# A hybrid decoder step on one core: two more buffers for the weight stream in the first two pieces of the input projection, and the next piece of the activations made ahead of the weight splits

## The chip, the cores and the metric

The kernel runs on one core of a Trainium2 chip. The metric is the device time of one execution in microseconds (us), as the median of several runs. In rows of the profile the engines are PE (TensorE, matrix products; PEld is its loading of weights), DVE (VectorE), ACT (ScalarE), POOL (GpSimd) and SP (SyncE, which here only issues DMAs). "SPq" and "POOLq" are the queues of DMAs that SP and POOL issue. "L675" is line 675 of the kernel before.

## The reference

One layer is computed for 264 tokens: a prompt of 256 and eight samples of one token each, D = 2048, all in float32. Cut to what matters here:

```python
mod = silu(c) @ w_ada + b_ada                     # (2048) @ (2048 x 12288)
sh1, sc1, gt1, sh2, sc2, gt2 = split(mod, 6)
h = rmsnorm(x, g_pre_mix) * (1 + sc1) + sh1
z = h @ w_in                                      # (264 x 2048) @ (2048 x 15376)
(z_uv, hq, hf, hi, ...) = split(z, ...)
...                                               # three mixers, gates, w_branch, w_out
x = x + gt1 * rmsnorm(out, g_post_mix)
h2 = rmsnorm(x, g_pre_mlp) * (1 + sc2) + sh2
y2 = square(relu(h2 @ w_mlp_up)) @ w_mlp_down
x = x + gt2 * rmsnorm(y2, g_post_mlp)
```

The point for this change is the order of the first lines: `h` needs `sh1` and `sc1`, two sixths of `mod`, and so 33.5 MB of `w_ada` before the first product with `w_in` is complete.

## The kernel before, in words

**Products in three passes.** A float32 product is made of three matmuls in a faster format. Each weight is split into a high part `whi` (ACT casts it, L631) and a low part `wlo` (DVE subtracts, L635). The activations are split in the same way into `hh` and `hl`. Lines L675, L676 and L677 then multiply `whi` by `hh`, `whi` by `hl` and `wlo` by `hh`.

**The stream.** All weights but `w_ada` come through one list of *granules* of 512 KB, loaded by DMAs that SP issues in the list's order (L616 for paired loads, L623 for single ones). A load waits until a buffer is free; the tag `raw` has four of them. `Stream.ahead`, called after each granule's matmuls, puts into the program the splits of the granule three places on (`SPLIT_AHEAD`) and the loads up to five places on (`LOAD_AHEAD`). A split can run when its load has landed and PE is through with the granule three places back. Two further buffers with the tag `araw` are used later, by paired loads and by `w_ada`.

**The first phase** makes 20 groups of 256 columns of `w_in`. As `h` isn't there at once, the 16 tiles of K are cut into five *pieces* of 2, 2, 4, 4 and 4 tiles (`CHUNKS`). Piece 0 runs over all 20 column groups with K tiles 0 and 1, piece 1 with tiles 2 and 3, and so on; the partial sums are added up in SBUF. A granule of pieces 0 and 1 is two K tiles by 512 columns, ten granules a piece, called g0 to g9 and g10 to g19 below; a granule of the later pieces is four K tiles by 256 columns, g20 and on. Each granule has two PSUM accumulators in pieces 0 and 1, and `evict` moves them to SBUF: in piece 0 ACT copies the first (L862) and DVE the second (L864), later DVE adds them (L110).

**Making the next piece.** While a piece runs, the class `First` prepares the activations of the next one as a generator (`paced`), resumed once after each granule by `next(nxt, None)` (L877). Its steps are: the `w_ada` matmuls in batches of four load units (L315, 1.9 us each), a copy of their sums to SBUF (`sums`, L319 on ACT), then `rows`: transposes on PE (L326), the sums to `mod` and `A1` on DVE (L110, L530), and at the next steps `modulate` for two K tiles at a time. `modulate` scales on ACT (L454, two instructions), computes the eight sample columns on POOL (L450, L451), casts the high part on ACT (L116) and subtracts for the low part on DVE (L113). The next piece's first matmul needs the cast.

**What sets the order.** In the first phase the order on all five queues is the order in which the program is written. After a granule's matmuls that is: its copies out, then the splits and the loads of `ahead`, then one step of the generator. `LOAD_AT` says at which granule each load unit of `w_ada` for the next piece is put into POOL's queue (256 KB per DMA for piece 1, 512 KB for the later ones, L502). POOL issues in order, so a load that stands behind L450 waits for it. A batch of `w_ada` matmuls is put in three granules (`ADA_LEAD`) after its last load unit was.

**The very first granule** has its own code: `modulate_first` computes the sample columns of the first two K tiles on POOL (L465 to L468), the rest on ACT (L471) and DVE (L472, L113), and `first_granule` (L689) uses them.

## Time and profile before

| what | us |
|---|---|
| median of 3 runs (1806.27 to 1812.08) | 1808.13 |
| the profiled execution's own time | 1805.63 |
| its span | 1803.9 |
| PE busy / DVE busy / ACT busy / POOL busy | 1775.1 / 1183.0 / 1001.4 / 138.7 |
| L675, L676 and L677 together | 3824.6 of overlapping matmuls |
| mean granted TensorE clock | 0.999 |

PE is busy for 98% of the span, and the chain of work that ended last is PE for 91% of it. So the kernel is bound by PE, and what can be won without taking work from PE is the sum of its gaps and the time in which its clock is lowered. The views to read are therefore the stages of the first phase in windows, and inside them the timeline of PE, with what ended each of its waits. DMA moved 442 MB at a mean of 245 GB/s over the span, but more than that in the first phase, where `w_ada` and `w_in` are fetched together.

### The profile page before, as it was taken

Reading aid. Unit: us, or ns where it says so; the run is one execution under the profiler, and the core shown is the slowest. Engines: PE = TensorE matmul, PEld = TensorE weight load, DVE = VectorE, ACT = ScalarE, POOL = GpSimd, SP = SyncE. Lnnn points to the kernel's source line nnn. Section 1 sums busy time; section 2 is a strip of 40 time slices with the busy share of each in tenths; the row PEclk is TensorE's granted clock in tenths of the full one; section 3 lists DMA queues with packets and bytes.
Section 4 is the critical chain, followed back from the end, with each engine's and each line's share of the span. In section 5 each row is a group of like instructions: output and inputs, shape, how many; then the busy total and the mean of one; then the engine's idle time right before and its main releaser. Section 6 shows DMA issues by size and latency. Waiting matters only on the chain.

```text
span 1803.9 us, 42121 instructions
## 1 busy us (share of the span) xinstructions
PE 1775.1 (98%) x16970; PEld 1687.9 (94%) x16970; DVE 1183.0 (66%) x2077; ACT 1001.4 (56%) x1824; POOL 138.7 (8%) x228
## 2 busy tenths in 40 slices
PE   7999999999999999999999999999999999999998
PEld 5889989999999989999999989999999999999997
DVE  5566667787687695566555667545666666666666
ACT  5344454677857765654444666555454545454554
POOL 4222000101101102110000010000000000000000
PEclk9999999999999999999999999999999999999999
DMA  9987587689689688887877946776666666666663
GB/s 339 387 338 282 197 291 253 208 293 304 211 281 302 218 276 303 306 311 257 289 262 253 327 140 203 240 248 221 192 196 198 196 193 197 196 193 196 199 191 116
DMA packets 330181, 442.05 MB, mean 245 GB/s; under 512 B 14947, under 2 KB 276945, under 8 KB 329985
## 3 DMA queue, kind: packets, MB, share of 16 engines
q1 hardware_dynamic: 311872, 380.52, 63.8%
q0 software_dynamic: 17184, 57.85, 9.4%
q8 instruction: 133, 2.18, 0.5%
q10 hardware_dynamic: 928, 0.99, 0.2%
q14 instruction: 64, 0.52, 0.1%
HBM read 427.60 MB, written 11.70 MB: 244 GB/s over the span
## 4 chain that ended last, share of the span: by engine, by line
PE 91%; DVE 1%; ACT 1%; issue 0%; DMA 0%; ACTq 0%; SPq 0%; DVEq 0%
PE mm L675 28%; PE mm L676 27%; PE mm L677 27%; PE ada L383 3%; PE ada L315 1%; PE sm L709 1%; PE sm L897 1%; PE sm L716 1%; DMA araw<-in_w_ada_dram 0%; DVE wlo L635 0%; PE sm L1622 0%; PE sm L1253 0%; DVE b L113 0%; DVE b L1602 0%; PE sm L1004 0%
## 5 line engine op out<-in xcount | busy, mean ns | idle before, releaser
L675 PE MATMUL mm<-b,whi 128*128 128x264 f32 x4600 | 1283.4, 279 | 4.8 <-ACT b L116 3.4
L677 PE MATMUL mm<-b,wlo 128*128 128x264 f32 x4600 | 1270.6, 276 | 1.1 <-DVE wlo L635 0.6
L676 PE MATMUL mm<-b,whi 128*128 128x264 f32 x4600 | 1270.6, 276 | 0.7 <-DVE b L113 0.7
L635 DVE TENSOR_TENSOR wlo<-raw,whi 128x512 fp32r<-128x512 f32 x1136 | 770.8, 689 | 463.4 <-ACT whi L631 460.2
L631 ACT CAST whi<-raw 128x512 fp32r<-128x512 f32 x1136 | 693.0, 617 | 672.4 <-DVE wlo L635 328.7
L675 PEld LDWEIGHTS mm<-b,whi 128*128 128x128 f32 x4600 | 870.1, 189 | 45.1 <-issue 23.3
L676 PEld LDWEIGHTS mm<-b,whi 128*128 128x128 f32 x4600 | 870.3, 189 | 1.4 <-DVE b L113 1.1
L677 PEld LDWEIGHTS mm<-b,wlo 128*128 128x128 f32 x4600 | 870.1, 189 | 1.5 <-DVE wlo L635 0.8
L110 DVE TENSOR_TENSOR b<-b,mm 128x528 f32<-128x528 f32 (+1 forms) x137 | 95.7, 699 | 74.6 <-PE mm L677 67.0
L1790 POOL TENSOR_TENSOR gs<-b,G 128x16 f32<-128x16 f32 x1 | 0.2, 223 | 714.1 <-DVE b L110 714.1
L502 POOL DMA_DIRECT2D b<-in_w_ada_dram x64 | 46.4, 727 | 39.2 <-PE ada L315 30.1
L383 PE MATMUL ada<-araw,cT 128*32 128x512 f32 x296 | 40.9, 601 | 0.8 <-DMA araw<-in_w_ada_dram 0.8
L1154 POOL DMA_DIRECT2D out_dram<-st x32 | 23.6, 737 | 223.7 <-DVE st L1153 223.7
L315 PE MATMUL ada<-b,cT 128*32 128x256 f32 (+1 forms) x640 | 34.5, 355 | 1.4 <-DMA b<-in_w_ada_dram 1.2
L1151 ACT ACTIVATE st<-st,fs 128x128 f32<-128x128 f32 (+1 forms) x96 | 35.1, 430 | 0.0
L1153 DVE SCALAR_TENSOR_TENSOR st<-vbc,b,st 128x128 f32<-128x128 f32 (+1 forms) x96 | 32.4, 390 | 3.7 <-DMA vbc<-vs_d 1.4
L107 DVE TENSOR_TENSOR b<-b,b 128x512 f32<-128x512 f32 (+1 forms) x47 | 33.8, 741 | 1.6 <-ACT b L1265 0.8
L315 PEld LDWEIGHTS ada<-b,cT 128*32 128x32 f32 x640 | 18.2, 114 | 12.6 <-DMA b<-in_w_ada_dram 4.1
L383 PE MATMUL ada<-b,cT 128*32 128x512 f32 x216 | 26.2, 593 | 0.0
L113 DVE TENSOR_TENSOR b<-gt,b 128x528 fp32r<-128x528 f32 x32 | 22.7, 708 | 3.2
L113 DVE TENSOR_TENSOR b<-b 128x1024 f32<-128x1024 f32 (+1 forms) x24 | 24.3, 1017 | 0.0
L1676 ACT ACTIVATE b<-vt 128x528 fp32r<-128x528 f32 x32 | 22.9, 714 | 1.0
(366 smaller groups left out, 902.7 us busy)
## 6 DMA issues: line engine op xcount, KB each, us to landing
raw<-in_w_in_dram SPq DMA_DIRECT2D x231, 512.0 KB, 5.1
raw<-in_w_mlp_up_dram SPq DMA_DIRECT2D x128, 512.0 KB, 3.7
raw<-in_w_mlp_down_dram SPq DMA_DIRECT2D x128, 512.0 KB, 3.5
araw<-in_w_ada_dram SPq DMA_DIRECT2D x74, 512.0 KB, 6.1
b<-in_w_ada_dram SPq DMA_DIRECT2D x54, 512.0 KB, 6.5
b<-in_w_ada_dram POOLq DMA_DIRECT2D x48, 512.0 KB, 10.5
raw<-in_w_branch_dram SPq DMA_DIRECT2D x48, 512.0 KB, 5.4
raw<-in_w_out_dram SPq DMA_DIRECT2D x32, 512.0 KB, 4.5
```

Source lines behind the costliest of these rows:

```text
L107: V.tensor_tensor(o, a, b, op=ALU.mult)
L110: V.tensor_tensor(o, a, b, op=ALU.add)
L113: V.tensor_tensor(o, a, b, op=ALU.subtract)
L315: T.matmul(acc[32 * j:32 * j + 32, 0:n], cT[:, k, :], w[:, n * j:n * j + n], start=k == 0, stop=k == KT - 1)
L383: T.matmul(self.acc[32 * j:32 * j + 32, :], cT[:, k, :], ws[j // 2][:, j % 2 * 512:j % 2 * 512 + 512], start=k == 0, stop=k == KT - 1)
L502: queue.dma_start(w[:, i], w1[k * P:(k + 1) * P, :, self.k0 * P:(self.k0 + self.n) * P])
L631: self.last = [S.copy(hi, raw).ins, None]
L635: self.last[1] = V.tensor_tensor(lo, raw, hi.bitcast(F32), op=ALU.subtract).ins
L675: T.matmul(o, a, xh(k + j), start=first and j == 0, stop=False)
L676: T.matmul(o, a, xl(k + j), start=False, stop=False)
L677: T.matmul(o, b, xh(k + j), start=False, stop=last and j == n - 1)
L1151: S.activation(st[:, i, :], st[:, i, :], AF.Copy, scale=fs[:, h0 + i, b:b + 1])
```

## The change

Four things are changed, all in the code of the first phase.

1. **Buffers.** In `Stream.load` every third granule of two K tiles (`n == 2 and i % 3 == 2`) takes a buffer of the tag `araw` in place of `raw`. With four `raw` and two `araw` that makes six. `Stream.ahead` loads seven granules ahead in place of five as long as the granule two further on is also one of two K tiles. Both conditions also hold for the eight granules of the first 512 columns of `w_mlp_up`.
2. **Order.** `granule` and `first_granule` take a function `between`, called ahead of `ahead()`. It advances the step and resumes the generator. So the generator's step now stands ahead of the splits and loads; the transposes of x (L282) stay behind them.
3. **Load table.** In `LOAD_AT`, the last three load units of piece 1 are put in one granule sooner. Those of piece 2 begin a granule later (7 in place of 6) and end a granule sooner (13 in place of 14). So the last batch of each piece, and with it `sums`, `rows` and `modulate`, comes a granule sooner.
4. **The first samples.** Two of the four small operations of `modulate_first` go from POOL to DVE.

```diff
 LOAD_AT = (
     (),
-    (0, 0, 1, 1, 2, 3, 4, 5),
-    (6, 6, 7, 8, 8, 9, 10, 10, 11, 11, 12, 12, 13, 13, 14, 14),
+    (0, 0, 1, 1, 2, 2, 3, 4),
+    (7, 7, 8, 8, 9, 9, 10, 10, 11, 11, 12, 12, 12, 13, 13, 13),
     tuple(range(16, 32)),
...
         hs, ls = (apart(b)[:, :, :, NP // 2:NT // 2] for b in (hi, lo))
-        Q.tensor_tensor(d, xs[:, 0:2, :], A[:, 0:2, 1:NC], op=ALU.mult)
-        Q.tensor_tensor(hs, by_two(d), by_two(B[:, 0:2, 1:NC]), op=ALU.add)
+        mul(d, xs[:, 0:2, :], A[:, 0:2, 1:NC])
+        add(hs, by_two(d), by_two(B[:, 0:2, 1:NC]))
         Q.tensor_tensor(d, d, B[:, 0:2, 1:NC], op=ALU.add)
...
-            t = rawp.tile([P, n, width], F32, tag="raw", name=nm("raw"))
+            if n == 2 and i % 3 == 2:
+                t = rawp.tile([P, n, width], F32, tag="araw", name=nm("araw"), bufs=ADA_RAW)
+            else:
+                t = rawp.tile([P, n, width], F32, tag="raw", name=nm("raw"))
...
-            for i in range(self.at + SPLIT_AHEAD + 1, min(self.at + LOAD_AHEAD + 1, end)):
+            last = self.at + LOAD_AHEAD
+            if self.items[min(last + 2, end - 1)][2] == 2:
+                last += 2
+            for i in range(self.at + SPLIT_AHEAD + 1, min(last + 1, end)):
                 if i not in self.raw:
                     self.load(i)
...
             if done:
                 done(acc0)
+        if between:
+            between()
         stream[0].ahead()
...
         for acc in accs:
             done(acc)
+        between()
         stream[0].ahead()
...
+            def between():
+
+                step[0] += 1
+                if not final:
+                    next(nxt, None)
+
             load_due()
             if ci or gi:
-                granule(win, 0, n, begin[gi * gn][0], gn * CW, accs, hH, hL, k0, True, True, evict)
+                granule(win, 0, n, begin[gi * gn][0], gn * CW, accs, hH, hL, k0, True, True, evict, between)
             else:
-                first_granule(accs, evict)
-            step[0] += 1
+                first_granule(accs, evict, between)
             if ci == 0 and 2 * gi + 8 < KT:
                 x_transposed(2 * gi + 8)
-            if not final:
-                next(nxt, None)
-            else:
+            if final:
```

**ACT at the end of piece 0.** Before, with `gt` the copy of the sums, `whi` the splits, `L862` the copies of g8 and g9 out of PSUM, and `L454`/`L116` the modulation for piece 1:

```order
L631 CAST whi_771<-raw_652 128x512
L319 COPY gt_809<-ada_580 128x128
L862 COPY b_177<-mm_811 128x528
L631 CAST whi_843<-raw_693 128x512
L631 CAST whi_847<-raw_693 128x512
L862 COPY b_179<-mm_857 128x528
L631 CAST whi_887<-raw_735 128x512
L631 CAST whi_891<-raw_735 128x512
L454 ACTIVATE b_271<-b_271,mod,A_169 128x256 x2
L116 CAST b_331<-b_271 128x528
```

And now (the line numbers are those of the changed kernel; L634 is L631, L871 is L862):

```order
L319 COPY gt_759<-ada_571 128x128
L634 CAST whi_761<-raw_481 128x512
L634 CAST whi_765<-raw_481 128x512
L871 COPY b_175<-mm_771 128x528
L634 CAST whi_807<-raw_531 128x512
L634 CAST whi_811<-raw_531 128x512
L871 COPY b_177<-mm_817 128x528
L454 ACTIVATE b_271<-b_271,mod,A_169 128x256 x2
L116 CAST b_331<-b_271 128x528
L634 CAST whi_855<-araw_612 128x512
L634 CAST whi_859<-araw_612 128x512
L871 COPY b_179<-mm_865 128x528
```

The modulation (L454, L116) stood behind the copy of g9 and two more splits; it now stands behind the copy of g8, ahead of the splits.

**POOL around the samples of piece 1.** The DMAs fetch `w_ada` for piece 2; L450 and L451 are the sample columns of the modulation. Before:

```order
L502 DMA b_813<-in_w_ada_dram 128x2x512
L502 DMA b_815<-in_w_ada_dram 128x2x512
L502 DMA b_859<-in_w_ada_dram 128x2x512
L450 TENSOR_TENSOR b_271<-xsn_132,A_169 128x2x8
L451 TENSOR_TENSOR b_271<-b_271,mod 128x2x8
L502 DMA b_905<-in_w_ada_dram 128x2x512
```

And now:

```order
L502 DMA b_819<-in_w_ada_dram 128x2x512
L502 DMA b_821<-in_w_ada_dram 128x2x512
L450 TENSOR_TENSOR b_271<-xsn_132,A_169 128x2x8
L451 TENSOR_TENSOR b_271<-b_271,mod 128x2x8
L502 DMA b_867<-in_w_ada_dram 128x2x512
L502 DMA b_869<-in_w_ada_dram 128x2x512
```

Of the sixteen loads of piece 2, six stood ahead of L450 (the first three aren't shown) and ten behind it; now four stand ahead (two aren't shown) and twelve behind.

**SP at the start of the stream.** Before, from the first granule on:

```order
L623 DMA raw_204<-in_w_in_dram 128x512 x2
L623 DMA raw_207<-in_w_in_dram 128x2x512
L623 DMA raw_209<-in_w_in_dram 128x2x512
L623 DMA raw_386<-in_w_in_dram 128x2x512
L623 DMA raw_388<-in_w_in_dram 128x2x512
L623 DMA raw_390<-in_w_in_dram 128x2x512
```

And now:

```order
L626 DMA raw_204<-in_w_in_dram 128x512 x2
L626 DMA raw_207<-in_w_in_dram 128x2x512
L626 DMA araw_209<-in_w_in_dram 128x2x512
L626 DMA raw_386<-in_w_in_dram 128x2x512
L626 DMA raw_388<-in_w_in_dram 128x2x512
L626 DMA araw_390<-in_w_in_dram 128x2x512
```

The order of the loads is the same, but the third and the sixth go to the two other buffers, so six loads can be out before the first buffer comes free, where it was four.

More of the change, by code (lines that the diff above doesn't have):

```diff
@@ L663, in hybrid_step_kernel, with granule @@
     stream = []
-    def granule(w, k0, n, c0, width, accs, xh, xl, k, first, last, done=None):
+    def granule(w, k0, n, c0, width, accs, xh, xl, k, first, last, done=None, between=None):
         item, parts = stream[0].next()
@@ L679, in granule, with first_granule @@
                 done(acc0)
+        if between:
+            between()
         stream[0].ahead()
-    def first_granule(accs, done):
+    def first_granule(accs, done, between):
         item, parts = stream[0].next()
```

## The prediction

> **What bounds the kernel now.** I read the page's busy times first, then the first phase in windows of 20 us, then PE's timeline in the windows that lose time, then the engines that PE waited for. The page says that PE is the bound, and so only its gaps and its clock can be won:
>
> ```profile
> PE 1775.1 (98%) x16970; PEld 1687.9 (94%) x16970; DVE 1183.0 (66%) x2077; ACT 1001.4 (56%) x1824; POOL 138.7 (8%) x228
> ```
>
> The windows (length, busy time of PE, PEld, DVE, ACT, POOL, then granted clock, DMA share, GB/s) show where they are:
>
> ```profile
> 20.00:40.00 20.00, 18.73 (x221) 16.45 (x225) 13.71 (x25) 11.68 (x22) 11.79 (x19) 1.00 0.97 357
> 40.00:60.00 20.00, 19.72 (x252) 19.00 (x241) 10.91 (x17) 9.60 (x19) 5.67 (x8) 1.00 1.04 404
> 60.00:80.00 20.00, 16.21 (x154) 13.71 (x153) 11.50 (x21) 7.01 (x13) 9.84 (x15) 0.91 0.97 362
> 80.00:100.00 20.00, 19.87 (x204) 17.57 (x203) 14.67 (x26) 8.22 (x15) 1.06 (x3) 1.00 0.79 301
> ```
>
> Two things stand in them. From 60 to 80 PE is idle for 3.8 us and its clock falls to 0.91; and up to 80 the DMA engines are full (share 0.97 and more), so whatever starts sooner takes bandwidth from something else. PE's timeline at the border of pieces 0 and 1 (start, duration, then in brackets the idle time before and who ended it):
>
> ```profile
> 58.77 0.28 PE L675 MATMUL mm<-b,whi 128*128 128x264 f32 x1
> ...
> 60.01 0.28 PE L677 MATMUL mm<-b,wlo 128*128 128x264 f32 x1
> 63.71 0.38 PE L675 MATMUL mm<-b,whi 128*128 128x264 f32 x1 [3.42 <-ACT b L116]
> 64.45 0.38 PE L676 MATMUL mm<-b,whi 128*128 128x264 f32 x1 [0.36 <-DVE b L113]
> ...
> 65.28 0.43 PE L677 MATMUL mm<-b,wlo 128*128 128x264 f32 x1
> ...
> 68.70 0.28 PE L677 MATMUL mm<-b,wlo 128*128 128x264 f32 x1
> ```
>
> The last matmul of g9 starts at 60.01, the last of g10 at 68.70. Matmuls at full clock follow each other every 0.113 us (58.77 to 60.01 are eleven steps), so the 24 of g10 should take 2.71; they took 8.69. The border costs 5.98 us: 3.42 and 0.36 of waiting, the rest from slow matmuls after it (0.43 against 0.28).
>
> [...]
>
> Why the cast L116 came so late is seen on ACT, DVE and POOL:
>
> ```profile
> 58.86 1.14 ACT L631 CAST whi<-raw 128x512 fp32r<-128x512 f32 x2 [1.79 <-DMA raw<-in_w_in_dram]
> 59.91 0.59 ACT L862 COPY b<-mm 128x528 f32<-128x528 f32 x1
> 60.77 1.14 ACT L631 CAST whi<-raw 128x512 fp32r<-128x512 f32 x2 [0.27 <-DMA raw<-in_w_in_dram]
> 61.82 1.09 ACT L454 ACTIVATE b<-b,mod,A 128x256 f32<-128x256 f32 x2
> 62.99 0.66 ACT L116 CAST b<-b 128x528 fp32r<-128x528 f32 x1
> 60.95 0.18 DVE L530 SCALAR_TENSOR_TENSOR A<-mod,vec 128x18 f32<-128x18 f32 x1
> 61.22 0.21 POOL L450 TENSOR_TENSOR b<-xsn,A 128x16 f32<-128x16 f32 x1 [13.31 <-DVE A L530]
> ```
>
> ACT first waits for two weight loads and splits them (58.86 to 61.9), then modulates. A1 (L530) is late for the same reason: it stands behind a DVE half of a split. So a wait for DMA is handed on, through two engines' queues, to PE.
>
> **The change part by part.** First the border. The two weight splits leave the path, and the chain starts a granule sooner. L326 and A1 come after g7, so A1 is ready about 4 us before PE is through with g9; ACT's L454 and L116 come behind g8's copy and take 1.09 + 0.66 = 1.75 us (from the rows above), and DVE's L113 follows. g8's first accumulator is full half a granule, 1.35 us, after g8 starts; with the copy (0.59) the cast is ready 3.7 us after that start, and PE wants it 5.4 after it (two granules). That leaves 1.7 us of cover: **gain 5.98 us**. The bounds are 5.98 (all) and 0 (the splits are still ahead of it in some way). What is queued behind: the split of g11 now waits for the modulation, 1.75 us; its granule is used two granules, 5.4 us, later, behind a batch of `w_ada`. And `sums` (L319) now holds ACT, ahead of a split, until the batch on PE is done; that split too is used three granules, over 8 us, later.
>
> The border of pieces 1 and 2 has a smaller copy of the same thing:
>
> ```profile
> 101.38 0.72 DVE L113 TENSOR_TENSOR b<-b,b 128x528 fp32r<-128x528 f32 x1 [0.38 <-ACT b L116]
> 102.86 0.35 PE L675 MATMUL mm<-b,whi 128*128 128x264 f32 x1 [0.73 <-DVE b L110]
> 105.25 0.38 PE L676 MATMUL mm<-b,whi 128*128 128x264 f32 x1 [0.36 <-DVE b L113]
> ```
>
> DVE waits with L113 for ACT's cast, the eviction L110 waits behind it, and PE for the eviction. Both pairs of tiles are now made a granule sooner: **gain 1.0** (0 to 1.09).
>
> The start: the first product waits for the samples from POOL and the scaled rows from ACT.
>
> ```profile
> 24.25 0.18 DVE L530 SCALAR_TENSOR_TENSOR A<-mod,vec 128x18 f32<-128x18 f32 x1
> 24.53 1.14 ACT L471 ACTIVATE b<-b,mod,A 128x256 fp32r<-128x256 f32 x2
> 24.59 0.21 POOL L465 TENSOR_TENSOR sqs<-xsn,A 128x16 f32<-128x16 f32 x1 [18.50 <-DVE A L530]
> 24.88 0.76 POOL L466 TENSOR_TENSOR b<-sqs,mod 128x16 fp32r<-128x16 f32 x1
> 25.69 0.49 PE L689 MATMUL mm<-b,whi 128*128 128x264 f32 x2 [0.40 <-ACT b L471]
> 24.87 0.68 DVE L635 TENSOR_TENSOR wlo<-raw,whi 128x512 fp32r<-128x512 f32 x1
> ```
>
> POOL ends at 25.64, ACT's first half at 25.1, so POOL was the later one, though the row names ACT. On DVE two operations of about 0.2 (as L530) end at 24.85, so PE can start at 25.1, 0.55 sooner. But DVE's own chain is pushed back by 0.4, and its `wlo` then ends at 25.95, where PE, four matmuls after its start, would want it at 25.55. **Gain 0.3** (-0.2 to 0.55).
>
> Now the costs: `w_ada` batches that PE reaches sooner than their loads land. The transposes, the batches on PE, and landing times (count, KB each, us from issue to landing; the first pair of rows is the DMAs issued at about 31.4 and 40.6, the eighth and the last of piece 1; then a weight load issued at 39.1; then loads of piece 2 issued at 62.0 and 71.4):
>
> ```profile
> 38.66 0.60 PE L282 MATMUL sm<-cst,b 128*128 128x128 f32 x4
> 39.19 1.96 PE L315 MATMUL ada<-b,cT 128*32 128x128 f32 x64
> 52.62 1.96 PE L315 MATMUL ada<-b,cT 128*32 128x128 f32 x64
> 91.29 1.93 PE L315 MATMUL ada<-b,cT 128*32 128x256 f32 x32
> ...
> 26.29 7.31 POOL L502 DMA_DIRECT2D b<-in_w_ada_dram  x10
> ```
>
> ```profile
> b<-in_w_ada_dram POOLq DMA_DIRECT2D x2, 256.0 KB, 8.8
> b<-in_w_ada_dram POOLq DMA_DIRECT2D x2, 256.0 KB, 8.0
> raw<-in_w_in_dram SPq DMA_DIRECT2D x1, 512.0 KB, 12.4
> b<-in_w_ada_dram POOLq DMA_DIRECT2D x1, 512.0 KB, 5.3
> b<-in_w_ada_dram POOLq DMA_DIRECT2D x2, 512.0 KB, 12.0
> ```
>
> Batch 1 of piece 1 needs its eighth DMA at three quarters of the 1.96 us, 40.65; it landed at 31.4 + 8.8 = 40.2, with 0.45 to spare. Now PE comes there 0.3 (start) and 0.53 (the transposes stand behind it) sooner, at 39.8. POOL starts its DMAs 0.9 sooner, as two operations (0.21 and 0.76) are gone. Against it stand two more weight loads of 0.52 MB in flight, 1.05 MB, at 404 GB/s (second window) up to 2.6 us. The wait is between 0 and 2.2. I take **0.5**: the window from 20 to 40 isn't full (357 against 404 GB/s, 0.9 MB), and that room nearly holds them.
>
> Batch 2 moves from 52.62 a granule sooner, to about 48.9 less what the start gained, and needs its last DMA at 50.4; it landed at 48.6. With the same shift it holds: 0 (0 to 0.8).
>
> Piece 2: of its loads twelve in place of ten stand behind L450, which moves from 61.2 to about 55. The first landed 5.3 after its issue, at 67.3; one of the last at 71.4 + 12.0 = 83.4. That is nine loads in 16.1 us, 293 GB/s. By that rate the twelve would land from 60.5 to 80.2; by what the window from 40 to 60 leaves `w_ada` (404 less four weight loads in 12.4 us, 169 GB/s: 235) until 85.1. PE reaches the last batch at 91.29 less 2.7 (a granule) less 6.3 (the shift), 82.3, and needs its last load at 83.7. The wait is 0 to 1.4; nearer the first, since the stream's six buffers are full by then and it only loads what is consumed: **0.5**.
>
> The MLP's eight granules are the last part. The two `araw` buffers are taken there by weights, and `w_ada` has to come after them:
>
> ```profile
> 959.41 0.34 SPq L346 DMA_DIRECT2D araw<-in_w_ada_dram  x1
> 1050.28 56.17 SPq L623 DMA_DIRECT2D raw<-in_w_mlp_up_dram  x14
> 1126.32 1.06 PE L383 MATMUL ada<-araw,cT 128*32 128x512 f32 x8
> ```
>
> This load was issued 167 us ahead of its use. It now comes behind about ten of these fourteen, at some 1095, 31 us ahead, and even 12.4 for landing leaves 19: 0. If that cover were gone, PE would wait there once.
>
> The sum: 5.98 + 1.0 + 0.3 - 0.5 - 0.5 = 6.3 us. The profiled execution took 1805.63 (its span 1803.9 and 1.7 around it), so it would take 1799.3. It is faster than every run shown; from the median, 1808.13, the same gain gives **1801.8**, 0.35% less. About 0.3%, 5.4 us, is what a measurement of this kernel tells from no change.
>
> **The rivals.** *The wait only moves.* The batches wait for their DMAs by the upper bounds, 2.2 + 0.8 + 1.4 = 4.4 in place of 1.0, and 2.9 are left: 1805.2. For it speaks the DMA share of 1.04, against it that from 80 to 100 the bus has room (share 0.79).
>
> *The stream takes the bus (slower).* Place: the last batch of piece 1, and then that of piece 2. With six weight loads in flight in place of four, 169 becomes up to 169 x 6/4 = 253, and 404 - 253 leaves 151 GB/s for `w_ada`. Eight DMAs of 0.262 MB took from 40.2 to 48.6, 250 GB/s; at 151 the second eight take 13.9, 5.5 later: 54.1 against 50.4, a wait of 3.7. Eleven loads of 0.524 MB behind the first, at 60.5 + 3.7, take 38.2 and end at 102, against 83.7 + 3.7: 15 more, with twice 1.8 of slow clock (0.09 of 20 us). The sum is 7.3 - 3.7 - 15 - 3.6, 15 slower: 1823. The point from which it decides is a share of `w_ada` of about 200 GB/s. Against it: the stream is held by its buffers, and once these are full it can't take more than PE consumes.
>
> [...]
>
> *The change doesn't do it.* ACT's splits of g9 and g10 still wait for DMA ahead of the modulation, and A1 is as late as before relative to PE. Then 0 to 1 is won: 1807.5. Against it: the six buffers put the loads two granules ahead.
>
> **How the numbers follow.** My forecast 0.60 (gain over 5.4); the wait only moves 0.18; the change doesn't do it 0.05; the stream takes the bus 0.17, of it 0.07 near equal turns with no difference and 0.10 slower. So faster 0.60, same 0.30, slower 0.10. The low end is all gains with no costs, 7.6, and 4 for the spread of the runs: 1796.5. The high end takes in the first and third rival and the mild form of the second: 1809.5.
>
> **What would show it.** Right: no wait on L116 at the border of pieces 0 and 1, g10 in 2.7 us, no slow clock after the start, no gap at the next border, the first L689 at about 25.1 to 25.4. Wrong: PE waiting at L315 for DMA `w_ada` for more than 2 us, or weight splits that wait longer for their loads than before.

## The result, and the profile after

| | before | after |
|---|---|---|
| median of 5 runs, us | 1808.13 | 1800.21 |
| lowest to highest, us | 1806.23 to 1812.08 | 1798.0 to 1801.41 |
| span of the profiled execution, us | 1803.9 | 1799.6 |
| the profiled execution's own time, us | 1805.63 | 1801.41 |

The changed kernel is faster: the ratio is 0.9959, with an interval of 0.9947 to 0.9971. The ratio is worth 7.4 us, between 5.2 and 9.6, and the two medians lie 7.9 apart. The prediction was 1801.8, in a range of 1796.5 to 1809.5.

Line numbers of the changed kernel are higher: L681, L682 and L683 are the L675, L676 and L677 of before; L634 and L638 are the splits L631 and L635; L871 and L873 the copies out of PSUM L862 and L864; L697 the first granule's L689. L110, L113, L116, L315, L450, L454 and L530 keep their numbers.

The first phase of the changed kernel, in the same windows of 20 us (length, busy time of PE, PEld, DVE, ACT, POOL, then granted clock, DMA share, GB/s):

```profile
20.00:40.00 20.00, 18.87 (x188) 16.62 (x187) 13.60 (x27) 12.71 (x25) 10.89 (x16) 1.00 1.05 400
60.00:80.00 20.00, 20.00 (x215) 17.26 (x217) 15.14 (x25) 8.29 (x15) 8.10 (x12) 1.00 1.02 391
```

From 60 to 80 PE was busy for 16.21 us at a clock of 0.91; it is busy for all 20.00 now, at 1.00. The first window moves 400 GB/s in place of 357, which is 0.86 MB more in 20 us.

The border of pieces 0 and 1, on PE (g9's last matmul, then the first and the last of g10, and the batch behind it) and on ACT, with A1 on DVE:

```profile
60.91 0.28 PE L683 MATMUL mm<-b,wlo 128*128 128x264 f32 x1
61.12 0.38 PE L681 MATMUL mm<-b,whi 128*128 128x264 f32 x1
...
63.81 0.28 PE L683 MATMUL mm<-b,wlo 128*128 128x264 f32 x1
64.01 0.64 PE L315 MATMUL ada<-b,cT 128*32 128x256 f32 x8
```

```profile
57.17 0.60 ACT L871 COPY b<-mm 128x528 f32<-128x528 f32 x1 [0.96 <-PE mm L683]
57.67 1.09 ACT L454 ACTIVATE b<-b,mod,A 128x256 f32<-128x256 f32 x2
58.85 0.68 ACT L116 CAST b<-b 128x528 fp32r<-128x528 f32 x1
56.55 0.18 DVE L530 SCALAR_TENSOR_TENSOR A<-mod,vec 128x18 f32<-128x18 f32 x1
```

g10 follows g9 without a wait: 2.90 us from g9's last matmul to g10's, in place of 8.69. The cast L116 is ready at 59.53, 1.6 us ahead of the matmul that wants it at 61.12. ACT now waits for PE ahead of its copy (0.96), and no longer for a load. Its longest waits from 27 to 65, the one before and then two after (line, who is waited for, us in total, times, longest):

```profile
ACT whi L631 <- DMA raw<-in_w_in_dram: 13.0, 8, 2.2
```

```profile
ACT b L871 <- PE mm L683: 8.4, 8, 3.3
ACT gt L319 <- PE ada L315: 2.7, 1, 2.7
```

Before, ACT waited for loads 8 times, 13.0 us in all; now only for PE.

What PE waits for from 26 to 110 in the changed kernel (line, who is waited for, us in total, times, longest):

```profile
PE mm L681 <- ACT b L871: 0.4, 1, 0.4
PE mm L681 <- DVE b L873: 0.3, 1, 0.3
PE mm L681 <- DVE b L110: 0.2, 1, 0.2
```

The first two stand at g1, ahead of its first and its second accumulator, right behind the start, and the second of them is new. No batch of `w_ada` waits for its loads.

**A measure that start and end do not blur.** The span fell by 4.3 us, and the median of the runs by 7.9. Two things lie between. A1 of the first piece, the end of all that happens before the first product, came at 25.38 in place of 24.25. And PE lost time in a place that the change doesn't touch: at 663.53 it waits for 2.01 us ahead of a matmul of L718, and the profile shows nothing that it waited for. Before, the same wait is 0.65. Over the thirteen profiles of this case the time from the fourth piece's first batch to the end of the span lies between 1693.6 and 1697.9 (1694.5 before, 1696.1 after, and the longest with the MLP's part undone), though nothing but that part acts there. So I compare kernels by a *stretch*: from A1 (the first L530) to the first `w_ada` batch of the fourth piece. All of the change but the MLP's loads acts inside it. Its end before (its start, 24.25, stands in the prediction), and then both ends after:

```profile
109.39 1.93 PE L315 MATMUL ada<-b,cT 128*32 128x256 f32 x32
```

```profile
25.38 0.18 DVE L530 SCALAR_TENSOR_TENSOR A<-mod,vec 128x18 f32<-128x18 f32 x1
103.53 1.93 PE L315 MATMUL ada<-b,cT 128*32 128x256 f32 x32
```

It is 85.14 before and 78.15 after: 6.99 us shorter, 6.02 of it up to the batch behind g10 (68.90 - 24.25 = 44.65 before, 64.01 - 25.38 = 38.63 after).

A wait in brackets is less than what it costs, as it counts only from the modelled end of the matmul before it. Ahead of the matmul at 49.72 in the kernel before the wait is 0.28, but that matmul starts 0.56 after the one ahead of it, in place of 0.11.

### The profile page after: what moved, and what is told of

Read it like the earlier page. It is cut to its first block, busy times and chain, and to the rows that moved or that the text cites. A ratio compares the mean times of both kernels' runs of the same rounds, so it can differ in the third digit from the quotient of the medians.

```text
span 1799.6 us, 42111 instructions
## 1 busy us (share of the span) xinstructions
PE 1774.1 (99%) x16970; PEld 1686.9 (94%) x16970; DVE 1183.5 (66%) x2079; ACT 1002.0 (56%) x1824; POOL 139.5 (8%) x226
## 4 chain that ended last, share of the span: by engine, by line
PE 93%; DVE 2%; DMA 2%; ACT 1%; issue 1%; SPq 0%; ACTq 0%; DVEq 0%
PE mm L681 28%; PE mm L682 28%; PE mm L683 28%; PE ada L383 3%; PE ada L315 1%; DMA raw<-in_w_in_dram 1%; DVE wlo L638 1%; PE sm L718 1%; PE sm L909 1%; PE sm L725 1%; DMA b<-in_x_prompt_dram 0%; ACT whi L634 0%; DVE b L113 0%; PE sm L1634 0%; DMA araw<-in_w_ada_dram 0%
## 5 line engine op out<-in xcount | busy, mean ns | idle before, releaser
L681 PE MATMUL mm<-b,whi 128*128 128x264 f32 x4600 | 1282.4, 279 | 1.6 <-ACT b L871 0.4
L683 PE MATMUL mm<-b,wlo 128*128 128x264 f32 x4600 | 1269.7, 276 | 1.5 <-issue 0.9
L682 PE MATMUL mm<-b,whi 128*128 128x264 f32 x4600 | 1269.6, 276 | 0.0
L638 DVE TENSOR_TENSOR wlo<-raw,whi 128x512 fp32r<-128x512 f32 x1118 | 759.8, 690 | 462.5 <-ACT whi L634 458.1
L634 ACT CAST whi<-raw 128x512 fp32r<-128x512 f32 x1118 | 682.8, 617 | 636.5 <-DVE wlo L638 319.8
L681 PEld LDWEIGHTS mm<-b,whi 128*128 128x128 f32 x4600 | 869.3, 189 | 42.1 <-issue 26.1
L682 PEld LDWEIGHTS mm<-b,whi 128*128 128x128 f32 x4600 | 869.6, 189 | 0.7 <-issue 0.5
L683 PEld LDWEIGHTS mm<-b,wlo 128*128 128x128 f32 x4600 | 869.4, 189 | 0.8 <-DVE wlo L638 0.8
L110 DVE TENSOR_TENSOR b<-b,mm 128x528 f32<-128x528 f32 (+1 forms) x137 | 95.7, 699 | 63.7 <-PE mm L683 55.8
L383 PE MATMUL ada<-araw,cT 128*32 128x512 f32 x296 | 40.9, 601 | 0.2 <-DMA araw<-in_w_ada_dram 0.2
L634 ACT CAST whi<-araw 128x512 fp32r<-128x512 f32 x38 | 23.2, 618 | 25.1 <-PE mm L682 21.7
L315 PE MATMUL ada<-b,cT 128*32 128x256 f32 (+1 forms) x640 | 35.4, 362 | 1.4 <-DMA b<-in_w_ada_dram 1.2
L315 PEld LDWEIGHTS ada<-b,cT 128*32 128x32 f32 x640 | 18.6, 116 | 13.2 <-DMA b<-in_w_ada_dram 4.1
L383 PE MATMUL ada<-b,cT 128*32 128x512 f32 x216 | 26.2, 593 | 0.0
L638 DVE TENSOR_TENSOR wlo<-araw,whi 128x512 fp32r<-128x512 f32 x38 | 24.6, 685 | 1.5 <-ACT whi L634 1.5
L113 DVE TENSOR_TENSOR b<-gt,b 128x528 fp32r<-128x528 f32 x32 | 22.7, 710 | 3.6 <-ACT whi L634 0.5
```

The lines of the kernel that those rows point to most:

```text
L110: V.tensor_tensor(o, a, b, op=ALU.add)
L315: T.matmul(acc[32 * j:32 * j + 32, 0:n], cT[:, k, :], w[:, n * j:n * j + n], start=k == 0, stop=k == KT - 1)
L383: T.matmul(self.acc[32 * j:32 * j + 32, :], cT[:, k, :], ws[j // 2][:, j % 2 * 512:j % 2 * 512 + 512], start=k == 0, stop=k == KT - 1)
L634: self.last = [S.copy(hi, raw).ins, None]
L638: self.last[1] = V.tensor_tensor(lo, raw, hi.bitcast(F32), op=ALU.subtract).ins
L681: T.matmul(o, a, xh(k + j), start=first and j == 0, stop=False)
```

## The experiments

The change has three parts that could have done this, and the prediction gave all the credit to what stands ahead of the modulation on ACT. (The first samples and the MLP's part were expected to do little, and are only undone below.) The *order theory* says: a part helps by as many instructions and waits as it takes from ahead of L454, up to the point where PE waits no more. The *buffer theory* says: the buffers do it, since ACT's waits for loads were the start of the delay. The runs: each part alone, the changed kernel with each part undone, and three further executions for the clock (1804.33 and 1805.57 us for the buffers alone, 1803.57 for the order alone, beside a single one of 1808.82 for the kernel before).

| kernel | median us (runs) | ratio to before, interval | stretch us |
|---|---|---|---|
| before | 1808.13 (5) | | 85.14 |
| changed | 1800.21 (5) | 0.9959 (0.9947 to 0.9971) | 78.15 |
| order alone | 1802.76 (6) | 0.9973 (0.9962 to 0.9985) | 80.76; again 81.45 |
| buffers alone | 1804.45 (11) | 0.9983 (0.9974 to 0.9992) | 83.18; again 81.84, 83.53 |
| load table alone | 1803.51 (10) | 0.9977 (0.9968 to 0.9986) | 80.78 |
| buffers undone | 1801.50 (5) | 0.9965 (0.9952 to 0.9977) | 80.06 |
| order undone | 1801.27 (5) | 0.9968 (0.9956 to 0.9981) | 79.64 |
| load table undone | 1801.50 (6) | 0.9969 (0.9958 to 0.9981) | 79.55 |
| first samples undone | 1799.72 (5) | 0.9960 (0.9947 to 0.9972) | 77.87 |
| MLP's part undone | 1800.11 (5) | 0.9960 (0.9946 to 0.9973) | 78.16 |

The ratios are to runs of the kernel before on the same chip, whose medians were 1807.21 (21 runs) for the parts alone and the buffers undone and 1807.66 (10 runs) for the other four. The intervals of the five kernels with one part undone all overlap that of the changed one, so the times can't rank them. The stretch comes from one profile each, and two executions of the same code differ in it (80.76 and 81.45; 81.84 to 83.53). So it is split at two points, the last matmul of g9 and the batch behind g10:

| kernel | A1 to g9's last matmul | from there to the batch behind g10 (border of pieces 0 and 1) | from there to the fourth piece's first batch |
|---|---|---|---|
| before | 35.76 | 8.89 | 40.49 |
| changed | 35.53 | 3.10 | 39.52 |
| order alone, two executions | 35.75; 35.16 | 5.87; 7.15 | 39.14; 39.14 |
| buffers alone, three | 35.21; 35.20; 35.21 | 7.48; 6.15; 7.81 | 40.49; 40.49; 40.51 |
| load table alone | 35.18 | 3.98 | 41.62 |
| buffers undone | 36.94 | 3.11 | 40.01 |
| order undone | 35.57 | 3.47 | 40.60 |
| load table undone | 35.54 | 4.87 | 39.14 |
| first samples undone | 35.25 | 3.11 | 39.51 |
| MLP's part undone | 35.53 | 3.13 | 39.50 |

### One part alone

**Order alone** (the kernel before, with `between` as in the change's diff; four buffers, old table, first samples on POOL):

```diff
+        if between:
+            between()
         stream[0].ahead()
...
```

> The kernel before with the order alone (generator step ahead of the splits). Two measures, in one profile each. The border: from the start of g9's last matmul to that of g10's last, 8.69 us before, 2.71 if nothing waits. The stretch: from A1 (first L530) to the first w_ada batch of the fourth piece, 85.14 before, 78.15 changed. Order theory (what counts is what stands on ACT ahead of the modulation): one split of the two is off the path, the cast follows the copy of g9 (end 60.5 in the rows before) by 1.75 us, at 62.3; PE waits about 2.1 in place of 3.42 and its clock is not lowered; border 4.9 to 5.3, stretch 81.0 (80.4 to 81.8), time about 1804. Buffer theory (without the two buffers ACT waits for loads as before, A1 and the cast stay as late): border 8 or more, stretch 84 or more, time 1807 to 1808.

PE waited 2.07 us for the cast and 0.36 for the low part, without a lowered clock (1.00 from 57.39 to 67.63), and the stretch is 80.76. ACT shows why it isn't less:

```profile
58.59 1.14 ACT L631 CAST whi<-raw 128x512 fp32r<-128x512 f32 x2 [2.00 <-DMA raw<-in_w_in_dram]
59.64 0.59 ACT L865 COPY b<-mm 128x528 f32<-128x528 f32 x1
60.13 1.09 ACT L454 ACTIVATE b<-b,mod,A 128x256 f32<-128x256 f32 x2
61.31 0.66 ACT L116 CAST b<-b 128x528 fp32r<-128x528 f32 x1
62.02 0.38 PE L675 MATMUL mm<-b,whi 128*128 128x264 f32 x1 [2.07 <-ACT b L116]
```

One split is gone from ahead of L454; the other, with its 2.00 us of waiting for a load, and the copy of g9 are still there. A1 was ready at 58.2, so it isn't what holds L454. The order theory's stretch and wait hold, and the buffer theory's (84 or more) do not. Its border was too short: from g9's last matmul to g10's it took 5.66 where 4.9 to 5.3 was expected, as the two waits cost more than their 2.07 and 0.36.

**Buffers alone** (the kernel before, with the second and third hunk of `Stream` as in the change):

```diff
+            if n == 2 and i % 3 == 2:
+                t = rawp.tile([P, n, width], F32, tag="araw", name=nm("araw"), bufs=ADA_RAW)
...
+            last = self.at + LOAD_AHEAD
+            if self.items[min(last + 2, end - 1)][2] == 2:
+                last += 2
...
```

> The kernel before with the six buffers and the deeper loading alone. Order theory: ACT no longer waits for loads, but one more split (1.14 us) and the copy of g9 still stand ahead of the modulation: copy at about 59.0 to 59.6, split to 60.8, cast at 62.5; PE waits 2.1 to 2.4, no lowered clock; border 4.9 to 5.5, stretch 81.5 (80.6 to 82.2), time about 1804.5. Buffer theory (the two buffers do it all): border 2.7 to 3, stretch 78.2 to 78.6, time 1800 to 1801.

ACT waits for no weight load any more, but both splits and the copy of g9 are ahead of L454, and PE waits for the cast all the same:

```profile
60.49 1.29 ACT L634 CAST whi<-raw 128x512 fp32r<-128x512 f32 x2
61.69 1.09 ACT L454 ACTIVATE b<-b,mod,A 128x256 f32<-128x256 f32 x2
62.86 0.67 ACT L116 CAST b<-b 128x528 fp32r<-128x528 f32 x1
63.58 0.54 PE L681 MATMUL mm<-b,whi 128*128 128x264 f32 x1 [2.34 <-ACT b L116]
64.32 0.59 PE L682 MATMUL mm<-b,whi 128*128 128x264 f32 x1 [0.20 <-DVE b L113]
```

The wait of 2.34 is what the order theory expected, and the buffers alone do not remove it. But the stretch is 83.18, outside its range (80.6 to 82.2): the matmuls behind the wait are slow (0.54 and 0.59), so the clock had fallen (to 0.50, at 63.66) after a wait of 2.34 us. A wait of 3.42, as in the kernel before, isn't needed for that. The last three runs take this up.

**Load table alone** (the kernel before with the two new rows of `LOAD_AT`):

```diff
-    (0, 0, 1, 1, 2, 3, 4, 5),
+    (0, 0, 1, 1, 2, 2, 3, 4),
...
```

> The kernel before with the load table alone. Order theory: the modulation stands behind the split that ended at 60.0 in the rows before, and ahead of the copy of g9 and the next split; cast at 61.75, PE waits about 1.6; border 4.3 to 4.7, stretch 80.5 (79.8 to 81.3), time about 1803.5. Buffer theory: 84 or more, time 1807 to 1808. By the order theory the gains of the three parts alone (about 4.1, 3.6 and 4.6 in the stretch) add up to far more than the 6.99 of all together, since each of them already takes the wait below the 3.4 us at which the clock fell.

The first border has one wait, of 0.68, for ACT's copy behind the cast. The cast was ready at 60.74, 35.6 us after A1, where I had worked out 37.5: the split ahead of L454 waited 0.23 for PE and not for a load. The stretch is 80.78, as expected, but by another road: two waits that I had not put in stand later.

```profile
86.99 0.64 PE L315 MATMUL ada<-b,cT 128*32 128x256 f32 x8 [1.38 <-DMA b<-in_w_ada_dram]
97.28 0.35 PE L675 MATMUL mm<-b,whi 128*128 128x264 f32 x1 [0.73 <-DVE b L110]
```

The first is the cost term that the prediction put at 0.5 for the changed kernel: with the load table alone, piece 2's loads behind L450 do come too late. So the load table alone shortens the first border by 4.91, more than either other part alone, and loses 1.13 behind it.

The three parts alone shorten the stretch by 4.4 (3.7 in a second execution), 1.6 to 3.3 and 4.4 us; together they shorten it by 6.99. They do not add up, because they work on one wait, and each takes away what stands ahead of the same two instructions.

### One part undone

**Buffers undone** (the changed kernel with the hunks of `Stream` taken back, four buffers and five granules ahead):

```diff
-            if n == 2 and i % 3 == 2:
-                t = rawp.tile([P, n, width], F32, tag="araw", name=nm("araw"), bufs=ADA_RAW)
-            else:
-                t = rawp.tile([P, n, width], F32, tag="raw", name=nm("raw"))
+            t = rawp.tile([P, n, width], F32, tag="raw", name=nm("raw"))
...
```

> The changed kernel without the two buffers and the deeper loading (order, load table and first samples as changed). Order theory: the modulation stands behind the copy of g8 alone, cast ready at about g9's end, border 2.7 to 3.0; but ACT waits for loads again (1.8 to 2.0 us ahead of each split, as before), so PE may wait for splits in the second piece: stretch 78.7 (78.1 to 80.2), time about 1800.8. Buffer theory: border 4 or more, stretch 81 or more, time 1804 or more. For the bus: with four weight loads in flight in place of six, a w_ada load of 256 KB should land in the same 8 to 9 us if six take nothing from w_ada, and in 6 to 7 us if the stream's share goes by its loads in flight.

The first border has no wait, so for it the buffers are not needed, and the buffer theory falls there. But the stretch is 80.06, 1.9 longer than with the buffers and near the far end of what I allowed. ACT waits for loads as before (7 times, 12.2 us from 27 to 65), and PE waits elsewhere:

```profile
35.93 0.38 PE L675 MATMUL mm<-b,whi 128*128 128x264 f32 x1 [0.38 <-ACT b L865]
47.19 0.38 PE L675 MATMUL mm<-b,whi 128*128 128x264 f32 x1 [0.25 <-ACT b L865]
84.77 0.64 PE L315 MATMUL ada<-b,cT 128*32 128x256 f32 x8 [0.29 <-DMA b<-in_w_ada_dram]
```

Twice here (and for 0.68 at g1, at 28.72) PE waits for ACT's copy out of PSUM. At 35.93 and 47.19 the copy stood in ACT's queue behind a split that had waited for its load, 3.26 us (34.24) and 1.96 us (45.50). So ACT's waits for loads cost PE time inside the first piece, not only at the border: 36.94 up to g9's last matmul in place of 35.53. A wait of 0.28 of this kind is in the kernel before too, at 49.72, and I had left it out of the sum. It comes and goes with four buffers: the order alone has it in one execution (0.34 at 49.39, and 35.75 up to g9) and not in the other (35.16), and the load table alone doesn't have it. None of the profiles with six buffers shows it.

For the bus, the landing times (count, KB, median us from issue to landing) of the loads issued from 33 to 42, with four weight loads in flight (buffers undone) and then with six (changed):

```profile
b<-in_w_ada_dram POOLq DMA_DIRECT2D x6, 256.0 KB, 8.1
raw<-in_w_in_dram SPq DMA_DIRECT2D x2, 512.0 KB, 12.5
```

```profile
b<-in_w_ada_dram POOLq DMA_DIRECT2D x8, 256.0 KB, 8.9
raw<-in_w_in_dram SPq DMA_DIRECT2D x2, 512.0 KB, 14.6
araw<-in_w_in_dram SPq DMA_DIRECT2D x1, 512.0 KB, 15.9
```

The deeper stream's own loads took longer, some 15 us in place of 12.5, and the loads of `w_ada` about as long as they had (8.9, against 8.1 here and 9.4 in the kernel before). What six buffers add, as far as the rows show, is an earlier start. From 26 to 28, when POOL has only begun to issue loads of `w_ada` (at 26.29 before, 26.95 in the changed kernel), four buffers leave the DMA engines half idle and six don't (before, then changed; DMA share and GB/s stand at the end):

```profile
26.00:28.00 2.00, 2.00 (x20) 2.00 (x19) 2.00 (x5) 2.00 (x5) 1.93 (x4) 1.00 0.45 163
```

```profile
26.00:28.00 2.00, 2.00 (x15) 1.56 (x15) 2.00 (x5) 2.00 (x5) 1.78 (x4) 1.00 1.05 409
```

In the same window it is 409 GB/s with the buffers alone, and 273 with the buffers undone.

**Order undone** (the generator's step behind `ahead()` again):

```diff
-        if between:
-            between()
         stream[0].ahead()
...
```

> The changed kernel with the generator step behind the splits again, buffers and table as changed. Order theory: one split (1.2 us) stands ahead of the modulation, but it waits for no load; cast at about 60.75 in the changed kernel's times, g10 starts at 61.12, so no wait for the cast and 0.3 for the low part L113; the second border loses the 1.0 it won; stretch 79.3 (78.6 to 80.7), time about 1801.3. If the order is needed whatever the buffers: a wait of 2 us at the first border, stretch 81 or more.

As the order theory expected: the cast ended at 60.81 and PE waited 0.17, for ACT's copy of an accumulator. The stretch is 79.64. At the second border the 0.73 of before is back (96.30, for DVE's L110), with 0.18 behind it, and a batch of `w_ada` waited 0.44. So once the buffers and the table are in, the order is worth 1.5 us, 0.37 of it at the first border and 1.08 behind it.

**Load table undone** (the two old rows of `LOAD_AT` in the changed kernel):

```diff
-    (0, 0, 1, 1, 2, 2, 3, 4),
+    (0, 0, 1, 1, 2, 3, 4, 5),
...
```

> The changed kernel with the old load table, buffers and order as changed. The cast stands behind the copy of g9 (end about 60.6 in the changed kernel's times), at 62.35, and PE is through with g9 at 61.1: a wait of about 1.2 and 0.36 for the low part, no lowered clock (1.6 idle of a window of 3.41); stretch 79.7 (79.2 to 80.3), time about 1801.8. If the granule sooner is not needed once the order is changed and nothing waits for loads: stretch 78.2 to 78.5.

PE waited 1.07 for the cast and 0.36 for the low part at the first border; the stretch is 79.55. The granule sooner is needed also when the order is changed and nothing waits for loads: without it the modulation stands behind g9's copy, which PE itself makes late. Of the three parts this one is needed most at the first border, 1.77 us. Behind that border the old table is better, 39.14 in place of 39.52.

**First samples undone** (the two small operations back on POOL):

```diff
-        mul(d, xs[:, 0:2, :], A[:, 0:2, 1:NC])
-        add(hs, by_two(d), by_two(B[:, 0:2, 1:NC]))
+        Q.tensor_tensor(d, xs[:, 0:2, :], A[:, 0:2, 1:NC], op=ALU.mult)
+        Q.tensor_tensor(hs, by_two(d), by_two(B[:, 0:2, 1:NC]), op=ALU.add)
```

> The changed kernel with the two small operations of the first samples back on POOL. The prediction's start term (0.3 gained): first product and g1 0.3 later against A1, stretch from A1 to the fourth piece's first batch 78.45 (78.15 changed). Rival (the term has the wrong sign: on DVE the two operations push back the low parts and the first copies): g1 starts 5.03 after A1 as before (5.08 changed), the wait of 0.34 for DVE's copy at g2 is gone, stretch 77.8 (77.6 to 78.0), time 1799.8. The times can't tell the two apart, the stretch can.

The stretch is 77.87, shorter by 0.28, so the rival holds: this part of the change costs a little. A difference of 0.28 between two executions is small, but the other profiles bear it out. Up to g9's last matmul the three with the two operations on DVE, no late copy and no lowered clock (changed, order undone, MLP's part undone) took 35.53 to 35.57. The six with them on POOL and no late copy took 35.16 to 35.25. DVE in the changed kernel and, below, with the two operations back on POOL:

```profile
25.59 0.18 DVE L107 TENSOR_TENSOR sqs<-xsn,A 128x16 f32<-128x16 f32 x1
25.80 0.18 DVE L110 TENSOR_TENSOR b<-sqs,mod 128x16 fp32r<-128x16 f32 x1
...
31.68 0.69 DVE L873 COPY b<-mm 128x528 f32<-128x528 f32 x1
```

```profile
24.43 0.18 DVE L530 SCALAR_TENSOR_TENSOR A<-mod,vec 128x18 f32<-128x18 f32 x1
24.72 0.41 DVE L472 TENSOR_SCALAR vt<-b,A,mod 128x256 f32<-128x256 f32 x1
...
30.33 0.71 DVE L873 COPY b<-mm 128x528 f32<-128x528 f32 x1
```

The first product starts 1.00 us after A1 in place of 1.45, but all that DVE does after it is later: the first granule's copy L873 starts 6.30 after A1 in place of 5.90, and PE waits 0.34 for it ahead of g1's second accumulator (what was expected above puts that wait at g2). The kernel with the first samples undone is the shortest in the stretch; by the medians (1799.72 and 1800.21) it can't be told from the changed one.

**The MLP's part undone** (both conditions limited to the first twenty granules):

```diff
-            if n == 2 and i % 3 == 2:
+            if n == 2 and i < 20 and i % 3 == 2:
...
-            if self.items[min(last + 2, end - 1)][2] == 2:
+            if last + 2 < 20:
```

> The changed kernel with both buffer conditions limited to the first two pieces, so that the MLP's first eight granules load as before. The prediction (that part costs nothing): stretch 78.15 within 0.3, the border of the MLP with the same two waits of about 0.76 and 0.74, time 1800.2 within 1.5. Rival (the later w_ada loads or the deeper stream win or cost something there): the stretch from the first L383 at that border to the end differs by over 0.3 us.

The stretch is 78.16. From the batch of L383 at the MLP's border to the end of the span it took 677.4 us (1123.48 to 1800.9), and 677.5 in the changed kernel (1122.14 to 1799.6). The MLP's part costs and gains nothing.

### The clock

**The buffers alone in two more executions, the order alone in one** (the same code as above):

> The kernel with the buffers alone once more, for the clock. In its first profile PE's wait of 2.34 us was enough to halve the clock, in the one with the order alone 2.07 and 0.36 were not. Grid theory: the clock is decided on a fixed grid of 3.413 us, whose phase is read from the drop behind the last matmul; it is halved for one grid step where the step before had PE busy for 1.1 us or less, and not where it was busy for 1.8 or more, whatever the length of the one wait. So with the same wait of about 2.3 the stretch from A1 to the fourth piece's first batch is 83.2 when the wait lies within one grid step and 81.4 when a step's border cuts it in two halves. Length theory (a wait over about 2.2 us halves the clock wherever it lies): 83.2 each time.

> As the run before it: the same kernel, at another phase of the grid.

> The kernel with the order alone once more. Grid theory: a wait of 2.07 and 0.36, 2.4 of idle in a stretch of 3.0; where the stretch falls within one grid step, PE is busy there for 1.0 us and the clock is halved (stretch about 82.3), else not (80.8). Length theory: never halved, 80.8.

In all thirteen profiles the clock also falls to 0.50 once PE has ended, behind the last matmul (at 1802.08 in the kernel before). In five of them the views also show it at 0.50 while PE still has work, each time for 3.41 us (3.413 in the kernel before, from 64.699 to 68.112). Steps of 3.413 us, counted back from the last fall; buffers alone, first execution (clock: third number from the end):

```profile
60.25:63.66 3.41, 1.07 (x10) 0.87 (x9) 2.42 (x7) 3.14 (x6) 2.42 (x5) 1.00 1.05 407
63.66:67.07 3.41, 3.21 (x13) 2.91 (x14) 0.61 (x1) 0.00 (x0) 3.09 (x5) 0.50 1.02 381
...
1804.46:1805.06 0.60, 0.00 (x0) 0.00 (x0) 0.00 (x0) 0.00 (x0) 0.00 (x0) 0.50 0.00 0
```

The two falls, at 63.66 and 1804.46, are 1740.80 us apart. In the kernel before (64.70 and 1802.08), in the third execution of the buffers alone (65.54 and 1802.92) and in the second of the order alone (63.49 and 1800.87) it is 1737.38, and in the load table undone (23.86 and 1798.79) 1774.93. That is 510, 509 and 520 steps, each within 0.1 of a step. So in these five the falls fit a fixed grid, and don't come when PE's wait begins or ends (in the kernel before the wait ended at 63.71, and the clock fell 0.99 later). The second execution of the buffers alone, with the same wait (2.35 us):

```profile
59.80:63.21 3.41, 2.16 (x20) 1.96 (x18) 2.79 (x7) 2.51 (x5) 1.25 (x4) 1.00 1.04 405
63.21:66.62 3.41, 1.96 (x15) 1.76 (x16) 1.43 (x4) 0.95 (x2) 3.41 (x5) 1.00 1.06 408
```

A border of the grid cuts the wait in two, PE is busy for 2.16 and 1.96 in the two steps, the clock stays at 1.00, and the stretch is 81.84. In the third the wait (2.35 again) falls so that one step has PE busy for 1.21; the clock is 0.50 in the next, and the stretch is 83.53. The order alone had 2.07 of waiting without a fall in its first execution (steps with 2.56 and 1.83). In its second:

```profile
60.08:63.49 3.41, 1.37 (x13) 1.17 (x11) 1.99 (x4) 3.32 (x7) 3.00 (x5) 1.00 1.05 407
63.49:66.90 3.41, 3.24 (x13) 2.94 (x14) 1.83 (x3) 0.93 (x2) 2.23 (x4) 0.50 1.01 371
```

The length theory said that it would never fall there; it fell after a wait of 2.04. The grid theory holds in these executions, with its limit moved from 1.1 to at least 1.37 us of busy time. Of the stretch it had said 82.3, and it was 81.45. The border did become 1.28 us longer than in the first execution (7.15 and 5.87); but up to g9's last matmul this one was 0.59 shorter, without the late copy of the first.

## Why the prediction was right, and where not

The time lies 1.6 us from the forecast, and the likeliest case was the right one. That it lies so near is in part luck: outside the stretch the profiles of this case differ by up to 4.3 us, and the errors of the terms have both signs. (The profiled execution itself took 1801.41, where the sum said 1799.3.) By its terms:

- **Border of pieces 0 and 1, gain 5.98: right, measured 5.79** (8.69 to 2.90; the forecast had 2.71, and g10's first two matmuls follow at 0.21, not at 0.11). Cast with 1.6 us of cover (predicted 1.7), A1 4.4 ahead of g9's last matmul (about 4), L450 at 56.82 (about 55, and the start was 1.13 later). That the buffers aren't needed at this border is shown by the buffers undone; that ACT's queue is the place, by its rows in the parts alone. Of the two things that the prediction credited, the granule sooner is the larger: without it the border loses 1.77, without the order 0.37.
- **Border of pieces 1 and 2, gain 1.0: right.** 6.99 less the 6.02 up to the batch behind g10 leaves 0.97; one wait of 0.2 is left, for DVE's L110. The order undone brings 0.73 and 0.18 back, so it is the order that won it. The granule sooner, which the prediction gave as the reason, did not: with the old table and the new order the gain is 1.35 (40.49 to 39.14, in three profiles), and the new table takes 0.38 of it back.
- **Start, gain 0.3: wrong sign, -0.28.** The step that failed: I priced DVE's delay of 0.4 only by the first granule's own matmuls and stopped there. The first product did come 0.45 sooner. But DVE was busy without a break from A1 to the copy of the first granule, and handed the delay on to g1, whose accumulators wait for copies.
- **Batches of `w_ada`, costs 0.5 and 0.5: neither came.** For piece 1 I set 1.05 MB more in flight against 0.9 MB of room in the first window; that window took 0.86 MB more and no batch waited. The step that failed for piece 2 is the landing rate, taken from between two bounds, 293 and 235 GB/s: from 68 to 80 us `w_ada` moved 3.24 MB, 270 GB/s, and no batch waited. That the term is real is shown by the table alone (1.38), the order undone (0.44) and the buffers undone (0.29).
- **What was left out, about 0.5.** ACT's copy was late once in the kernel before already (0.28 at 49.72). Up to g9's last matmul the change won 0.23 with the start's -0.28 in it, so 0.51 without. Part of this is the luck of one execution, as the same wait is missing from two profiles with four buffers. Taking the buffers away from the changed kernel costs 1.9 in the stretch, in one profile, much more than I would have given for them.
- **The clock.** The sum holds, since no wait is left at the first border. That a wait cut to about 2 us leaves the clock as it is, on which the expectations of the order and the buffers alone counted, was an estimate, and it does not hold in general: with 2.07 the clock stayed at 1.00, with 2.04 it fell to 0.50.

The terms as they were: 5.79, 0.51 and -0.28, together 6.02, and 0.97, against a forecast sum of 6.3; so the gain is 6.99 in the stretch, and 7.9 by the medians.

**The rival of the slower sign rested on a wrong step.** It let the stream's share of the bus grow with its loads in flight, 169 x 6/4. The queues' packets and bytes say otherwise; from 46 to 52 us, before and then after (q0 carries POOL's loads of `w_ada`, q1 SP's stream):

```profile
q0 software_dynamic: 438, 1.59, 66.0%
q1 hardware_dynamic: 447, 0.86, 37.9%
```

```profile
q0 software_dynamic: 444, 1.61, 66.2%
q1 hardware_dynamic: 445, 0.86, 37.2%
```

Four or six loads in flight, the two queues move about the same number of packets, and the same bytes. It isn't that the stream asked for no more: in the kernel before, ACT's splits wait for its loads in this very window (1.94 at 51.61). `w_ada` had 1.6 MB in 6 us, 265 to 268 GB/s, not 151. Nor was the split before 169 to 235: by these bytes it was 143 to 265. The milder form of this rival, near equal turns with no difference in time, has 0.07 of the chances and a part in the high end of the range; no run shows an equal split of the bandwidth. What the runs showed is near equal numbers of packets (444 and 445), and as q0's packets are larger (3.6 KB against 1.9, bytes by packets), `w_ada` got about two thirds (1.61 MB of 2.47). With that worked out ahead, the 0.17 of this rival would have been near nothing, and the two cost terms smaller. Nor did the wait only move (0.18), and the change did what it says (0.05 against it).

## What to carry to other kernels

When a small chain (a transpose, a scale, a cast) feeds the bound engine and stands in the same in-order queue as prefetch work with longer lead, put it ahead of that work, let its inputs come sooner, and look for what its queue waits for; several remedies for one wait do not add up, so price them together, up to where the wait is zero. An operation moved off a slower engine (one of the two here took 0.76 us on POOL and takes 0.18 on DVE) must be priced on the engine it goes to until that engine first has a gap, not only up to the first consumer. Here more loads in flight took no bandwidth from another queue that had work too (`w_ada` got 265 GB/s with four and 268 with six, from 46 to 52), and helped by filling a stretch in which the other queue had hardly begun (409 GB/s in place of 163, from 26 to 28); count packets per queue to see who gets what.

## What the hardware showed that I had not expected

- The falls of TensorE's clock fit a fixed grid of 3.413 us (509, 510 or 520 steps apart in one execution, in the five that show one while PE still has work). At the border of pieces 0 and 1, a step with PE busy for 0.63 (before), 1.07, 1.21 or 1.37 us was followed by one at 0.50; steps with 1.83 (order alone) or 1.96 (buffers alone, second execution) were not. The same wait of 2.35 us cost about 1.7 us more in one execution than in another, by its phase alone (83.53 and 81.84). Busy time as the profile counts it isn't the whole measure: in the load table undone, a step at the start had PE busy for 2.02 with the small matmuls of L315, and the clock was 0.50 in the next.

```profile
20.45:23.86 3.41, 2.02 (x41) 0.68 (x39) 0.49 (x1) 0.43 (x2) 0.00 (x0) 1.00 1.07 393
23.86:27.27 3.41, 3.41 (x14) 3.23 (x15) 2.80 (x9) 2.83 (x6) 1.84 (x4) 0.50 1.05 407
```

- Two DMA queues that both have work moved nearly equal numbers of packets (444 and 445 in 6 us), so bytes went by packet size (1.61 MB and 0.86), and the deeper queue got longer landing times for itself (some 15 us a load in place of 12.5) and not share.
